# Another order of steps in both attention layers and in the third mixer, and transpositions in place of identity matmuls for spread statistics

## The chip, the cores and the metric

The kernel runs on one core of one Trainium2 chip. The metric is the device time of one execution, in microseconds (us). The core has five engines that run their own instruction streams and meet at semaphores: TensorE (PE; its weight loads are shown apart as PEld), VectorE (DVE), ScalarE (ACT), GpSimd (POOL) and SyncE (SP, which here issues the DMAs). An operand of a matmul lies in SBUF, its result in a bank of PSUM.

## What is computed

Two transformer blocks over 256 tokens of width 1024, in float32. The first has two layers; the token mixer of each holds a banded attention (a), a sparse attention with compressed keys, chosen blocks and a window (b), and a gated delta rule (c). The second has a spatial gate beside a dilated attention, a cross attention to a memory of 256 rows, and a feed-forward network on either side.

```python
def hybrid_layer(x, c, ...):
    mod = jax.nn.silu(c) @ ada_w + ada_b
    sh_m, sc_m, gt_m, sh_f, sc_f, gt_f = jnp.split(mod[:, None, :], 6, axis=-1)
    h = rms_norm(x, norm_mix) * (1 + sc_m) + sh_m
    ...
    o_a = banded_attention(...)
    o_b = nsa_mixer(...)
    o_c = gated_delta_net(cqkv, ca, cb, cz, conv_w, A_log, dt_bias, gdn_norm)
    x = x + gt_m * (jnp.concatenate([o_a, o_b, o_c], axis=-1) @ w_out)
    h = rms_norm(x, norm_ffn) * (1 + sc_f) + sh_f
    gate, up = jnp.split(h @ w_gate_up, 2, axis=-1)
    return x + gt_f * ((jax.nn.silu(gate) * up) @ w_down)
...
def second_block(x, mem, positions, ...):
    h = rmsnorm(x, ffn1_norm[l])
    x = x + 0.5 * swiglu(h, ffn1_w_gate[l], ffn1_w_up[l], ffn1_w_down[l])
    h = rmsnorm(x, mix_norm[l])
    z = h @ w_in[l]
    ...
    y_a = chunked_spatial_gating(z_sgu, sgu_ln_g[l], sgu_ln_b[l], sgu_w_s[l], sgu_b_s[l])
    y_b = dilated_mixture_attention(q, k, v).reshape(b, s, D_ATT)
    y = jnp.concatenate([rmsnorm(y_a, out_norm_a[l]), rmsnorm(y_b, out_norm_b[l])], axis=-1)
    x = x + y @ w_out[l]
    ...
```

## The kernel before

**Projections.** The weights lie in memory as float32 blocks (`in_wbig`). SP fetches one block after another into a few buffers named `raw`; ACT rounds it to `hi` (L397), DVE takes the rest as `lo` (L398), and every product is made of three matmuls, hi by hi, hi by lo and lo by hi (`mm3`, L440, which issues through `mm`, L438). The activations are kept as such a pair too (`hhi`, `hlo`), transposed, with tokens along the free axis. Projections write PSUM tiles named `psw`, the rest `psb` and `psi`.

**Norms.** Squares are summed by one-column matmuls (`sqs`), DVE and POOL turn the sums into reciprocal roots (`rstd`, L456: L458 on DVE, the power L459 on POOL, tile `trs`), and `spread` (L529) lays the two columns of 128 tokens out over all 128 partitions: each column, broadcast along the free axis, is the stationary operand of a 128x128 float32 matmul by the identity. The result scales the blocks of the next norm (`norm_block`, L541). It runs eight times: in the start for the memory and the first norm, at the three feed-forward networks that use it, before the second layer, and twice around 815 us for the second block (once on a tile `r`).

**The conditioning vector.** `c_row` (L677) does the same with the eight columns of `ccol` in the start, for the row that DVE multiplies into the weights of `ada` (L685, L689; these products are spread over layers 0 and 1).

**The attention layers.** `mixer` (L804) writes each part as a generator of steps and runs them in the order of a string, `SEQ` (L275; `next(steps[c])` at L913). The letters: 0 to 3 heads of the delta rule up to its triangular system, t the token-wise projections, i the rounds of the triangular inverse, x and y the two halves of `delta_out` (L1049), c the compression, r the rotations (`rope`, L1166), m the compressed branch (L1223), a the banded attention (`window`, L1261), b the chosen and windowed branch (`selected`, L1326), z the projection `gated` (L874) with the norm of the delta rule's output behind it, p the output projection, A the products of `ada`, L loads of constants and v a value projection of the memory. In `window` the probabilities `sa` are divided by their sums on DVE (L1295) and transposed (L446); `selected` does so with `sb` (L1360); both are then copied out of PSUM on ACT (L1302, L1311, L1373, L1380) and multiplied by the values. `delta_out` ends with a norm (tile `so`: L1089, L458, the power L459 on POOL, L1091) and a copy by ACT to `oc` (L1095).

The order of the string is not the engines' order as such. It is the order in which instructions are written, and with it the order in which buffers and PSUM banks are handed out. A scheduler then places each instruction on its engine as its model thinks its operands ready, with the earlier written first. The orders below are the outcome.

**The third mixer.** `mixer2` (L1490) does the same with another string (L1667): g a projection with gelu or the values, a scores, b transposition of probabilities, p values, s the spatial gate, k the key's rotation, t the transposition of the gate's half. There PE's order is fixed to the written one (`pe_order`).

## Time and profile before

| | |
|---|---|
| runs | 1369.58, 1364.94, 1365.35 us |
| median | 1365.35 us |
| the profiled execution's own time | 1370.71 us |
| its span | 1368.9 us |
| mean granted clock of TensorE | 0.988 |
| DVE busy | 984.0 us (72%) |
| ACT busy | 723.1 us (53%) |
| POOL busy | 42.6 us (3%) |
| DMA, mean | 202 GB/s |

The profile's own execution is the longest of those shown. What is read from it is set against its own 1370.71 us; 1.8 us of that lie outside the span. In rows of a timeline a matmul's duration reaches beyond the start of the next one, since matmuls are pipelined; the pace is read from start to start. A name that is repeated behind an arrow (`psi<-constt,trs`) is output, then stationary and moving operand; `constt` holds the identity and other constants.

### The profile page before, as it was taken

What the parts mean: (1) busy time and instruction counts of PE and PEld (TensorE: products, weight loads), DVE (VectorE), ACT (ScalarE), POOL (GpSimd) and SP (SyncE); (2) the same over time, 40 slices, a digit from 0 to 9 for tenths busy, and PEclk for the clock granted to TensorE, in tenths of its full rate; (3) what the DMA queues carried; (4) which work ended last, traced back from release to release, by engine and by line L of the source; (5) the groups of instructions that cost most, each with busy time, mean ns of one, the idle gap of its engine ahead of it and who ended that gap; (6) DMA issues with size and microseconds to landing.
All of it is one profiled execution on the core that took longest, in us unless ns stands there. A gap on an engine that the chain in (4) does not pass through costs nothing.

```text
span 1368.9 us, 27046 instructions
## 1 busy us (share of the span) xinstructions
PE 1319.0 (96%) x10952; PEld 1261.3 (92%) x10952; DVE 984.0 (72%) x1817; ACT 723.1 (53%) x1349; POOL 42.6 (3%) x47
## 2 busy tenths in 40 slices
PE   6899999999999999999999999999999999999998
PEld 5888879999999988799999989999987999999997
DVE  6878887999886888657666676665676664655554
ACT  4486384655445853855444454444466654544442
POOL 1001000000000000000000000000001000000000
PEclk9999999999999999899999999999999999999999
DMA  8876747799984564147666535555653543555551
GB/s 281 308 266 218 286 153 289 270 346 330 305 276 141 180 213 151 63 139 235 199 215 214 186 129 195 185 185 185 208 184 130 200 156 108 169 185 185 185 185 47
DMA packets 79037, 276.75 MB, mean 202 GB/s; under 512 B 9152, under 2 KB 9920, under 8 KB 78912
## 3 DMA queue, kind: packets, MB, share of 16 engines
q1 hardware_dynamic: 78912, 275.02, 58.7%
q8 instruction: 86, 1.41, 0.4%
q14 instruction: 39, 0.32, 0.1%
HBM read 271.31 MB, written 3.15 MB: 200 GB/s over the span
## 4 chain that ended last, share of the span: by engine, by line
PE 67%; issue 15%; DVE 7%; ACT 5%; DMA 4%; POOL 2%; SPq 0%; DVEq 0%; POOLq 0%; ACTq 0%
PE psw L438 40%; PE psb L438 21%; DMA raw<-in_wbig_dram 3%; PE psi L438 2%; PE psb L446 2%; DVE lo L398 2%; PE psi L1008 1%; DVE raw L689 1%; ACT hi L397 1%; POOL trs L459 1%; DVE hlo L558 1%; ACT s L1628 1%; DMA xres<-in_x_dram 1%; DVE xres L714 0%; PE psb L1131 0%
## 5 line engine op out<-in xcount | busy, mean ns | idle before, releaser
L398 DVE TENSOR_TENSOR lo<-raw,hi 128x1024 fp32r<-128x1024 f32 (+1 forms) x392 | 476.5, 1219 | 189.2 <-ACT hi L397 179.6
L397 ACT ACTIVATE hi<-raw 128x1024 fp32r<-128x1024 f32 (+1 forms) x392 | 409.6, 1052 | 346.7 <-PE psw L438 185.7
L438 PE MATMUL psw<-hhi,hi 128*128 128x256 f32 (+1 forms) x1744 | 499.4, 287 | 3.9 <-ACT hi L397 2.6
L438 PE MATMUL psw<-hhi,lo 128*128 128x256 f32 (+1 forms) x1744 | 497.2, 286 | 1.0 <-DVE lo L398 1.0
L438 PE MATMUL psw<-hlo,hi 128*128 128x256 f32 (+1 forms) x1744 | 497.1, 285 | 0.2 <-DVE hlo L558 0.2
L438 PEld LDWEIGHTS psw<-hhi,hi 128*128 128x128 f32 x1744 | 332.3, 191 | 6.8 <-ACT hi L397 3.5
L438 PEld LDWEIGHTS psw<-hhi,lo 128*128 128x128 f32 x1744 | 332.8, 191 | 2.5 <-DVE lo L398 1.9
L438 PEld LDWEIGHTS psw<-hlo,hi 128*128 128x128 f32 x1744 | 333.4, 191 | 1.5 <-DVE hlo L558 0.6
L438 PE MATMUL psb<-fhi,lo 128*128 128x256 f32 x704 | 197.1, 282 | 0.0
L438 PE MATMUL psb<-flo,hi 128*128 128x256 f32 x704 | 196.9, 281 | 0.0
L438 PE MATMUL psb<-fhi,hi 128*128 128x256 f32 x704 | 194.9, 282 | 0.1
L438 PEld LDWEIGHTS psb<-flo,hi 128*128 128x128 f32 x704 | 133.1, 189 | 0.2
L438 PEld LDWEIGHTS psb<-fhi,lo 128*128 128x128 f32 x704 | 132.8, 189 | 0.0
L438 PEld LDWEIGHTS psb<-fhi,hi 128*128 128x128 f32 x704 | 131.3, 189 | 0.9 <-ACT fhi L478 0.9
L689 DVE CUSTOM_DVE_ANT_0 raw<-raw,constt 128x1024 f32<-128x1024 f32 x96 | 116.2, 1218 | 0.0
L478 ACT ACTIVATE fhi<-fa 128x256 fp32r<-128x256 f32 x88 | 36.7, 417 | 112.3 <-DVE fa L758 59.5
L438 PE MATMUL psb<-oT,hi 128*128 128x256 f32 x512 | 92.7, 283 | 0.0
L438 PEld LDWEIGHTS psb<-oT,hi 128*128 128x128 f32 x512 | 79.0, 189 | 0.3
L438 PE MATMUL psb<-oT,lo 128*128 128x256 f32 x256 | 71.9, 281 | 0.0
L438 PE MATMUL psw<-lo,hhi 128*128 128x256 f32 (+2 forms) x208 | 68.8, 332 | 0.8 <-DVE lo L398 0.8
L438 PE MATMUL psw<-hi,hhi 128*128 128x256 f32 (+2 forms) x208 | 69.5, 336 | 0.0
L438 PE MATMUL psw<-hi,hlo 128*128 128x256 f32 (+2 forms) x208 | 67.9, 329 | 0.0
(364 smaller groups left out, 1549.2 us busy)
## 6 DMA issues: line engine op xcount, KB each, us to landing
raw<-in_wbig_dram SPq DMA_DIRECT2D x498, 512.0 KB, 4.3
mem<-in_mem_dram SPq DMA_DIRECT2D x8, 256.0 KB, 6.6
raw<-in_wbig_dram SPq DMA_DIRECT2D x4, 414.0 KB, 3.4
xres<-in_x_dram SPq DMA_DIRECT2D x4, 256.0 KB, 6.6
memd<-memk SPq DMA_DIRECT2D x4, 256.0 KB, 7.8
mk<-memd SPq DMA_DIRECT2D x4, 256.0 KB, 4.9
mv<-memd SPq DMA_DIRECT2D x2, 512.0 KB, 6.8
out_dram<-out SPq DMA_DIRECT2D x4, 256.0 KB, 2.5
```

Of the source, the lines that this page charges most:

```text
L397: a = self.nc.scalar.activation(hi[:, :n], r, AF.Copy)
L398: d = self.nc.vector.tensor_tensor(lo[:, :n], r, hi[:, :n].bitcast(F32), op=OP.subtract)
L438: return self.pe(self.nc.tensor.matmul(out, lhsT, rhs, start=start, stop=stop))
L446: self.pe(self.nc.tensor.transpose(out, in_, self.cc("ident")))
L459: self.nc.gpsimd.tensor_tensor(dst, dst, self.mhalf[:, :n], op=OP.pow)
L478: self.nc.scalar.activation(hi, src, AF.Copy)
L558: self.nc.vector.scalar_tensor_tensor(lo(m), x, s, hi(m).bitcast(F32), op0=OP.mult, op1=OP.subtract))
L689: self.ada_last = self.nc.vector.tensor_tensor_reduce(w, w, self.crow, 1.0, 0.0, OP.mult, OP.add, m[:, j:j + 1])
L1008: self.pe(self.nc.tensor.matmul(out[h, uh[u]], lhsT(h, u), rhs[h, uh[u]], start=True, stop=True, tile_position=(h.start, h.start)))
L1628: last["exp"] = act.activation(s2[:, o], s2[:, o], AF.Exp, bias=mx[:, i:i + 1], accum_out=sums[t][:, h:h + 1])
```

## The change

Three edits: the two strings of `SEQ`; `mm(..., ident)` against `tr` in `spread` and `c_row`, so that the broadcast column becomes the input of a TensorE transposition with the identity, the instruction that L446 issues elsewhere; and the string of `mixer2`.

```diff
-SEQ = {0: "0tLtttt0t001L11L12012223323A33iiiiciiiiiiciiicixyxycrcxyrArrAAAxyrrAArrmrabbAaaaabbbmbbbbAbbbzzAAzzAAzzApppAApApApAApAAAA",
-       1: "vtttvtv0vtt000111021122333332c2iciiiiiiiiiriiicicrrxyrrrrxyxyaxyacrrbmmbaAbaAAAbAbAzAbabAbzzbbbzzbzppppppp"}
+SEQ = {0: "0tLtttt0t001L11L12012223323A33iiiiciiiiiiciiicixyxyccyxrryrAAxrrrAAAArrmrabbabAaaabbbbmbbAbbzzbAAzzAAzzAppApAApApAApAAAAp",
+       1: "tvvtttv0vtt000111021221233332c3iciiiiiiiiiriiicicrrxyrrxyrraxyxyacrrbmmbaAbaAbAbAAAzAbabAbzzbbbzzbppzppppp"}
...
     def spread(self, r):
...
         p = self.pi()
         for t in range(2):
-            self.mm(p[:, t * 128:t * 128 + 128], r[:, t:t + 1].to_broadcast([128, 128]), self.cc("ident"))
+            self.tr(p[:, t * 128:t * 128 + 128], r[:, t:t + 1].to_broadcast([128, 128]))
...
     def c_row(self):
...
-                self.mm(p[:, i * 128:i * 128 + 128], self.ccol[:, 4 * h + i:4 * h + i + 1].to_broadcast([128, 128]), self.cc("ident"))
+                self.tr(p[:, i * 128:i * 128 + 128], self.ccol[:, 4 * h + i:4 * h + i + 1].to_broadcast([128, 128]))
...
-        for c in "ggkgggagagagabgbsgabgabsgbgtbpp":
+        for c in "ggggkgagagagabsgabgbgabsggbbptp":
```

Three places show how the engines' orders move. A number behind a name tells buffers apart and is not the same before and after.

The first is on PE, behind `delta_out` in layer 1 (about 559 to 571 us of the profile before). `kb,qb` are scores of the selected branch, `sa` and `sb` the transpositions, `psw<-hhi` and `psw<-hlo` the z projection. Before:

```order
L438 MATMUL psb_7168<-kb_7070,qb_7077 128x512
L438 MATMUL psb_7169<-kb_7070,qb_7077 128x512
L446 MATMUL psb_7184<-constt,sa_1451_6953 128x128
L446 MATMUL psb_7184<-constt,sa_7030 128x128
L446 MATMUL psb_7184<-constt,sa_1451_6953 128x128
L446 MATMUL psb_7184<-constt,sa_7030 128x128
L438 MATMUL psb_7215<-kb_7070,qb_7077 128x512
L438 MATMUL psb_7216<-kb_7070,qb_7077 128x512
L446 MATMUL psb_7299<-constt,sb_7085 128x128
L438 MATMUL psw_7235<-hlo_5454,hi_7318 128x256
```

After:

```order
L438 MATMUL psb_7209<-kb_7070,qb_7077 128x512
L438 MATMUL psb_7210<-kb_7070,qb_7077 128x512
L438 MATMUL psw_7235<-hhi_5453,hi_7238 128x256
L438 MATMUL psw_7235<-hlo_5454,hi_7238 128x256
L438 MATMUL psw_7235<-hhi_5453,lo_7239 128x256
L438 MATMUL psw_7235<-hhi_5453,hi_7238 128x256
L438 MATMUL psw_7235<-hlo_5454,hi_7238 128x256
L438 MATMUL psw_7235<-hhi_5453,lo_7239 128x256
L438 MATMUL psb_7281<-k0T_7163,vt_5504 64x256 x2
L438 MATMUL psb_7281<-k1T_7151,vt_5504 64x128 x2
L446 MATMUL psb_7299<-constt,sb_7085 128x128
L438 MATMUL psw_7235<-hhi_5453,hi_7318 128x256
```

Between the last scores and the first `sb` there were no matmuls of the projection, and now there are six, with the product of `k0T` and `k1T`. Of the 28 that were issued ahead of `delta_out`, 13 stay there, 5 lie inside it and the rest behind. The eight small products of the compressed keys (`kcf,qc`) that stood ahead of `delta_out` now stand right behind it.

The second is on PE, behind `delta_out` in layer 0 (about 188 to 194 us of the profile before). Before, transpositions of `sa` alternate with the z projection:

```order
L446 MATMUL psb_2306<-constt,sa_2279 128x128
L438 MATMUL psw_2461<-hlo_672,hi_2464 128x256
L438 MATMUL psw_2461<-hhi_671,lo_2465 128x256
L446 MATMUL psb_2313<-constt,sa_2282 128x128
L446 MATMUL psb_2313<-constt,sa_484_2208 128x128
L446 MATMUL psb_2313<-constt,sa_2282 128x128
L438 MATMUL psw_2461<-hhi_671,hi_2464 128x256
L438 MATMUL psw_2461<-hlo_672,hi_2464 128x256
```

After, from the last products of `delta_out` on:

```order
L438 MATMUL psi_1986<-u_370_1785,qk_729 128x128
L446 MATMUL psb_2316<-constt,sa_2276 128x128 x2
L446 MATMUL psb_2322<-constt,sa_2276 128x128
L446 MATMUL psb_2316<-constt,sa_2279 128x128
L446 MATMUL psb_2322<-constt,sa_483_2205 128x128
L446 MATMUL psb_2316<-constt,sa_2279 128x128
L446 MATMUL psb_2322<-constt,sa_2276 128x128
L446 MATMUL psb_2329<-constt,sa_2279 128x128
L446 MATMUL psb_2329<-constt,sa_484_2208 128x128
L446 MATMUL psb_2329<-constt,sa_2279 128x128
L446 MATMUL psb_2387<-constt,sb_2300 128x128
L438 MATMUL psw_2449<-hhi_671,lo_2453 128x256
```

All transpositions of `sa` stand in one run now. Behind them come nine matmuls of the projection, and then a run of eight transpositions of `sb`: the first four read `sb_2231` and `sb_2300`, the fifth `sb_2347`.

The third is DVE's order at the same place, which makes `sa` and `sb` ready. Before:

```order
L1295 TENSOR_SCALAR sa_2279<-sa_2279,sm_2271 128x256
L1091 SCALAR_TENSOR_TENSOR so_2014<-so_2014,rr_154_733 128x4
L458 TENSOR_SCALAR so_2038<-so_2038 128x4
L1295 TENSOR_SCALAR sa_2279<-sa_2279,sm_2271 128x256
L1091 SCALAR_TENSOR_TENSOR so_2038<-so_2038,rr_161_740 128x4
L1295 TENSOR_SCALAR sa_2282<-sa_2282,sm_2271 128x256 x2
```

After:

```order
L1295 TENSOR_SCALAR sa_2276<-sa_2276,sm_2268 128x256 x2
L1295 TENSOR_SCALAR sa_2279<-sa_2279,sm_2268 128x256 x2
L1089 TENSOR_TENSOR so_1931<-so_1931,so_412_1932 128x4
L1358 TENSOR_TENSOR smb_2302<-smb_2302,sg_723 128x2
L1356 RECIPROCAL smb_2349<-smb_2349 128x2
L458 TENSOR_SCALAR so_1931<-so_1931 128x4
L1360 TENSOR_SCALAR sb_2300<-sb_2300,smb_2302 128x256
L1091 SCALAR_TENSOR_TENSOR so_1931<-so_1931,rr_161_740 128x4
L1360 TENSOR_SCALAR sb_2300<-sb_2300,smb_2302 128x256
L1358 TENSOR_TENSOR smb_2349<-smb_2349,sg_723 128x2
L689 ISA raw_2526,mod_97<-raw_2526,constt 128x1024
L689 ISA mod_97 128x1
```

The four divisions of `sa` no longer stand between the steps of the norm `so`; the divisions of `sb` do (L1360), and one of the large products of `ada` (L689) and the next row of `so` stand ahead of the first division of `sb_2347`.

## Prediction

> **What bounds the kernel now.** First the page: busy time by engine, and the clock that TensorE was granted in 40 slices.
>
> ```profile
> PE 1319.0 (96%) x10952; PEld 1261.3 (92%) x10952; DVE 984.0 (72%) x1817; ACT 723.1 (53%) x1349; POOL 42.6 (3%) x47
> PEclk9999999999999999899999999999999999999999
> ```
>
> PE is busy for 1319.0 of 1368.9 us. All that the change can win back lies in the 49.9 us between, in PE work that becomes cheaper, and in stretches at a lower clock. Next the busy time of the engines by stretch (the columns are the stretch, its length, busy time and count of PE, PEld, DVE, ACT and POOL, the granted clock, the DMA share and GB/s): layer 0's attention, layer 1's, the end of it, and the third mixer.
>
> ```profile
> 60.00:216.00 156.00, 148.43 (x1412) 129.13 (x1412) 128.68 (x350) 105.71 (x263) 7.73 (x8) 1.00 0.67 233
> 440.00:560.00 120.00, 117.01 (x1201) 107.08 (x1201) 101.30 (x254) 73.04 (x184) 5.50 (x5) 1.00 0.53 177
> 560.00:575.00 15.00, 11.94 (x52) 7.15 (x52) 10.61 (x69) 11.61 (x48) 1.49 (x2) 0.66 0.03 12
> 1005.00:1081.00 76.00, 73.66 (x407) 60.41 (x405) 54.45 (x129) 53.09 (x100) 6.68 (x7) 1.00 0.47 159
> ```
>
> The reordered stages leave PE idle for 7.6 us (layer 0), 3.0 and 3.1 us (layer 1) and 2.3 us (third mixer), 16 us in all, and only the 15 us from 560 on run at a low clock. Then PE's waits by what ended them: total, times, longest.
>
> ```profile
> PE psi L438 <- POOL trs L459: 9.5, 7, 2.0
> ...
> PE psb L446 <- ACT s L1628: 0.8, 1, 0.8
> PE psb L446 <- ACT va L1566: 0.6, 1, 0.6
> ```
>
> The largest, the wait for the power on POOL, stands ahead of `spread`, and a transposition waits for it as a matmul does. I count it as unchanged.
>
> **The spreads.** These are the rows of PE (start, duration) at three of the eight, with the row behind each. Those at 250 and 621 us are like the first, the one at 1173 like the second; the last two lie in the start, where PE waits for weights.
>
> ```profile
> 440.03 0.71 PE L438 MATMUL psi<-constt,trs 128*128 128x128 f32 x4 [1.60 <-POOL trs L459]
> 440.50 0.36 PE L438 MATMUL psw<-oT,lo 128*128 128x256 f32 x1
> ...
> 814.93 1.22 PE L438 MATMUL psi<-constt,trs 128*128 128x128 f32 x4 [1.50 <-POOL trs L459]
> 815.80 0.56 PE L438 MATMUL psw<-hhi,lo 128*128 128x256 f32 x1
> ...
> 821.68 0.61 PE L438 MATMUL psi<-constt,r 128*128 128x128 f32 x4
> 822.04 0.36 PE L438 MATMUL psw<-hlo,hi 128*128 128x256 f32 x1
> ```
>
> Two matmuls of a spread leave four records: float32 goes through in two passes. From its start to the next matmul a spread takes 0.47 us at full pace (0.36 at 821.68), and 0.87 where PE runs at half pace. A transposition of a float32 block leaves one record:
>
> ```profile
> L446 PE MATMUL psb<-constt,sb x48: 270/273/448, 189.2 to 583.4; 128*128 128x128 f32 x48
> 194.00 0.71 PE L446 MATMUL psb<-constt,sb 128*128 128x128 f32 x5
> ```
>
> Five take 0.71, one 0.27, so the pace is (0.71 - 0.27) / 4 = 0.11 us, that of one pass: 0.47 / 4 = 0.12. Two transpositions replace four passes, and each spread falls to half. At full pace that saves (3 x 0.47 + 0.36) / 2 = 0.88 us, at half pace 2 x 0.87 / 2 = 0.87. Behind each stands a projection matmul on a PE that is never idle long, so this is on the path: **-1.8 us**. The bounds are 0, if a transposition of a broadcast column takes two passes after all, and -2.7 us, if the two in the start, at 0.87 each, count as well.
>
> **The conditioning vector.** Eight matmuls in 16 passes, and the row behind them:
>
> ```profile
> 8.97 3.75 PE L438 MATMUL psb<-constt,ccol 128*128 128x128 f32 x16 [8.97 <-DMA constt<-in_consts_dram]
> 13.14 0.58 PE L438 MATMUL psw<-oT,hi 128*128 128x256 f32 x1 [0.42 <-ACT hi L397]
> ```
>
> Half of 3.75 is 1.9 us of PE time, but the matmul behind waits for ACT's `hi`, so what hides this edit is the first weight's load and split. I take 0. If that cover went, it would be -1.9; of ACT's two copies of the result one stands behind that `hi` now, and if it comes ahead of it, `hi` is late by 0.6:
>
> ```profile
> 12.05 1.04 ACT L397 ACTIVATE hi<-raw 128x1024 fp32r<-128x1024 f32 x1
> 13.00 0.58 ACT L683 ACTIVATE constt<-psb 128x512 f32<-128x512 f32 x1
> ```
>
> **Layer 1.** The rows of PE behind `delta_out`, the place whose orders are shown with the change:
>
> ```profile
> 560.33 0.93 PE L446 MATMUL psb<-constt,sa 128*128 128x128 f32 x7
> 561.90 1.91 PE L438 MATMUL psb<-kb,qb 64*128 64x512 f32 x4 [0.64 <-ACT oc L1095]
> 565.42 1.11 PE L446 MATMUL psb<-constt,sa 128*128 128x128 f32 x4 [1.61 <-ACT oc L1095]
> 566.47 2.08 PE L438 MATMUL psb<-kb,qb 64*128 64x512 f32 x4
> 569.36 0.45 PE L446 MATMUL psb<-constt,sb 128*128 128x128 f32 x1 [0.81 <-DVE sb L1360]
> ...
> 570.03 0.42 PE L438 MATMUL psw<-hhi,hi 128*128 128x256 f32 x1
> 570.24 0.41 PE L438 MATMUL psw<-hlo,hi 128*128 128x256 f32 x1
> ```
>
> Three waits add up to 3.06 us, and the projection goes at 0.21 us a matmul, half its pace elsewhere. What the projection issued earlier (28 matmuls ahead of `delta_out`) is missing here. The change keeps 15 of them back. At full pace a matmul of it takes 0.12 us from start to start:
>
> ```profile
> 199.07 0.28 PE L438 MATMUL psw<-hhi,lo 128*128 128x256 f32 x1
> 199.19 0.28 PE L438 MATMUL psw<-hhi,hi 128*128 128x256 f32 x1
> ```
>
> 15 x 0.12 = 1.8 us that are no longer spent ahead of `delta_out`, where the inverse's last rounds have rotations and transpositions for cover instead, and that now fall into 3.06 us of waiting: **-1.8 us**. The wait for `sb` (0.81) is where six of them stand. The two waits for `oc` I leave: they come from ACT, which is busy for 11.61 of these 15 us and gets the same work, and the norm's power on POOL lies on the way. The bounds: with all three waits gone and the clock full, 3.06 us, and from 564.3 to 574.5 half of PE's 8.27 busy us there, 4.1 more, so -7.2; and, if the cover ahead of `delta_out` is too thin, the 1.8 us come back as a wait with half of a like low-clock stretch behind it, +3.5.
>
> ```profile
> 564.30:574.50 10.20, 8.27 (x32) 5.24 (x32) 8.09 (x49) 8.75 (x36) 0.00 (x0) 0.50 0.00 1
> ```
>
> **Layer 0.** First PE's two waits for `sa`:
>
> ```profile
> 191.18 0.33 PE L446 MATMUL psb<-constt,sa 128*128 128x128 f32 x1 [0.57 <-DVE sa L1295]
> 192.54 0.60 PE L446 MATMUL psb<-constt,sa 128*128 128x128 f32 x3 [0.79 <-DVE sa L1295]
> ```
>
> Then DVE's rows behind them, one product of `ada`, and the busy time of a stretch a little later (DVE is the third pair):
>
> ```profile
> 190.63 0.16 DVE L1091 SCALAR_TENSOR_TENSOR so<-so,rr 128x4 f32<-128x4 f32 x1 [0.90 <-POOL so L459]
> 192.14 0.61 DVE L1295 TENSOR_SCALAR sa<-sa,sm 128x256 f32<-128x256 f32 x2
> 198.29 1.21 DVE L689 CUSTOM_DVE_ANT_0 raw<-raw,constt 128x1024 f32<-128x1024 f32 x1
> ```
>
> ```profile
> 196.00:200.00 4.00, 4.00 (x34) 3.04 (x31) 4.00 (x12) 4.00 (x13) 0.00 (x0) 1.00 0.87 304
> ```
>
> DVE stood at L1091 for POOL, with divisions of `sa` queued behind. The change writes these ahead of it: 0.57 + 0.79 = 1.36 us go. What is queued behind L1091 now is `sb_2300`'s second division, then a product of 1.21 us, then `sb_2347`. From the first division of `sa` DVE needs 4 x 0.3 for `sa`, 0.2 for small steps, 0.3 for the first of `sb_2300`, 0.9 at L1091, 0.3, 1.21 and 0.3, in all 4.4 us, before the fifth transposition of PE's run can go. PE has 16 transpositions at 0.11 and nine matmuls at 0.12 ahead of it, 2.8 us, and starts them 0.3 behind DVE: a wait of about 1.3 us. Farther on `sb_2363` is transposed with no matmul of the projection beside it. DVE is busy without a gap there (4.00 of 4.00 us) and its work isn't less, so PE can't be past the last `sb` much sooner than before, whatever it wins at `sa`: a second wait between 0 and 1.9 us, of which I take 0.6, a third, as the 27 matmuls ahead of it are cover. -1.36 + 1.3 + 0.6 = **+0.5 us**. Bounds: -1.4, and +3.0 if the waits are 2.5 (DVE's product and its wait, 0.9 + 1.21, with PE early by 0.4) and 1.9. A rearranged fetch (the second half of a compression weight ahead of two `ada` blocks in SP's queue) falls within these.
>
> **The rest.** In the third mixer transpositions of `s` and the values' projection trade places; its waits of 0.8 and 0.6 can go or double: 0, from -1.4 to +1.4. The first matmuls of the two feed-forward networks behind the layers shift by one to nine places around `sqs`, below 1 us either way.
>
> **The sum**: -1.8 - 1.8 + 0.5 = -3.1. The profiled execution, 1370.71 us, would become 1367.6. It is 5.4 us above the median of the runs shown, 1365.35, and the same -3.1 there gives **1362.2 us**. A measurement of this kernel can tell about 0.5%, 6.8 us, from no change; the forecast is well within that.
>
> **A rule on the clock.** Here is PE in layer 0 where `sa` is transposed between waits:
>
> ```profile
> 190.00:193.00 3.00, 1.65 (x13) 1.18 (x12) 1.44 (x8) 2.13 (x9) 1.60 (x2) 1.00 0.95 343
> 812.00:824.00 12.00, 10.43 (x66) 10.17 (x67) 7.73 (x14) 5.71 (x9) 3.38 (x2) 0.72 0.61 218
> ```
>
> PE is busy for half of these 3 us, some of that with transpositions, and the clock stays at 1.00. The second row is a place where a wait was followed by half pace: 0.28 of 12 us below full, so a price of 3.4 us. The Trainium skill, "TensorE: Matmul & The Clock Gate", Part 4 on the PE-mode transpose, says that a transposition doesn't count as busy PE for the clock gate. By that rule each run of transpositions of this change is like a wait. The row at 190 doesn't bear it out, though it doesn't refute it either, as seven matmuls stand among them.
>
> **The rivals.**
> 1. *Layer 1's low clock goes as well.* Six projection matmuls and the product of `k0T` between the scores and the first `sb` keep PE at work; for it speaks that a third of the stretch's waiting was there; against it, the 1.61 us wait for `oc` that came first, and whose cause stays. Then -7.2 takes the place of -1.8: 1356.8 us. Chance 0.19.
> 2. *Layer 0 turns slower.* One mechanism: DVE divides `sb` behind the norm's wait for POOL and the products of `ada`, and PE comes to the new runs of transpositions with nothing else to issue. It decides from the point where PE gets there over 1.5 us ahead of DVE, about what preceded the half pace at 814.93. Then 2.5 and 1.9 us of waits, less 1.4, are +3.0, and two stretches at half pace add 6.8; layer 1 gains nothing: 1365.35 - 1.8 + 3.0 + 6.8 = 1373.4. For it: DVE's 4.4 us against PE's 2.8. Against it: DVE often runs ahead of PE there. Chance 0.10.
> 3. *Runs of transpositions lower the clock.* With one stretch at half pace in layer 0 and no new wait, 1362.2 + 3.4 = 1365.6 us. Chance 0.07. This is what the skill's rule would bring.
> 4. *The change doesn't do what it says*: a broadcast column is transposed in two passes, as many as before, and the orders only trade one wait for another: 1365.4. Chance 0.12.
> 5. The forecast, from 1359 to 1366: 0.52.
>
> **How the numbers follow.** The likeliest is 1362.2. Leaving out the far tails of rivals 1 and 2 gives 1356 to 1371. Faster by over 0.5% means under 1358.5: rival 1, mostly, with a tail of the forecast, 0.20. Slower by over 0.5% means over 1372.2: most of rival 2 and little beside it, 0.09. The rest is 0.71.
>
> **What would show it.** The spread: two records at L446 in place of four at L438, and 0.24 us (0.44 at half pace) to the next matmul; 0.47 refutes the first term. Layer 1: no wait for `sb` around 566, the projection's matmuls in its place; if the stretch is as long as before, or PE waits between the inverse and `delta_out`, the second term is wrong. Layer 0: no waits for `sa`, one of about 1 us for `sb` some 3 us later; a wait over 2 us, or a granted clock below 1.00 between 190 and 216 us, means rival 2. The forecast is wrong altogether if stretches that it doesn't speak of, the third mixer above all, change by over 1.5 us.

## The result, and the profile after

| | before | after |
|---|---|---|
| median of 4 runs each | 1367.46 us | 1349.07 us (1347.76 to 1350.83) |
| ratio, 95% interval | | 0.9865 (0.9837 to 0.9894) |
| span of the profiled execution | 1368.9 us | 1347.9 us |
| mean granted clock in it | 0.988 | 0.995 |

The kernel became 18.4 us faster, 1.35%. The forecast was 1362.2 us, with a range from 1356 to 1371: the measured time lies below all of it. The page of the changed kernel, its busy time and the granted clock in 40 slices:

```profile
PE 1303.4 (97%) x10928; PEld 1250.6 (93%) x10928; DVE 982.3 (73%) x1817; ACT 723.4 (54%) x1349; POOL 38.9 (3%) x47
PEclk9999999999999999999999999999999999999999
```

DVE and ACT do what they did. PE is busy 15.6 us less although only 24 of its records are gone, and POOL 3.7 us less, which no edit intended. Both are clues: work of the same kind goes faster.

A part of that is TensorE's clock. In every trace it stands at half for stretches of 3.41 us, or two or three times that, and at full otherwise. Ahead of PE's last matmul such stretches add up to 30.7 us in the profile before and to 10.2 after. Work at half clock takes twice as long, so half of the difference, about 10 of the 21.0 us between the two spans, can be the clock's (less where PE waited in them anyway). A profile is one execution; by the granted clock that is recorded for each, (1 - clock) x span fell from 15.8 us (11 of the kernel before, mean clock 0.9885) to 7.6 (six of the changed kernel, 0.9943, run e16 below): up to 8 us.

This table of PE's time from one spread to the next, read from the start of their rows in both traces, says where the 21.0 us are:

| stretch | before | after | difference |
|---|---|---|---|
| layer 0, attention | 214.5 | 208.3 | -6.2 |
| first network, up to layer 1's norm | 189.9 | 189.5 | -0.4 |
| layer 1, attention | 181.1 | 173.9 | -7.2 |
| second network | 193.8 | 193.6 | -0.2 |
| between the spreads at 815 and 822 us | 6.8 | 5.6 | -1.2 |
| third network, third mixer, cross attention | 350.9 | 348.4 | -2.4 |
| last network to PE's last matmul | 189.7 | 186.6 | -3.1 |

Apart from the last spread's passes the last network and the stretch ahead of it were in no term of the forecast; a change of over 1.5 us in such a stretch was one of its own signs of being wrong. PE's waits after the change, of the kinds that the prediction spoke of (total, times, longest):

```profile
PE psi L446 <- POOL trs L459: 7.8, 7, 1.6
...
PE psb L446 <- DVE sb L1360: 0.9, 1, 0.9
```

The waits for `sa` (L1295) and for `oc` (L1095) are in no row any more. Two places that were forecast, a spread and the conditioning vector, each with the row behind it (start, duration):

```profile
433.55 0.43 PE L446 MATMUL psi<-constt,trs 128*128 128x128 f32 x2 [0.94 <-POOL trs L459]
433.74 0.37 PE L438 MATMUL psw<-oT,hi 128*128 128x256 f32 x1
```

```profile
9.75 1.94 PE L446 MATMUL psb<-constt,ccol 128*128 128x128 f32 x8 [9.75 <-ACT oT L557]
14.53 0.80 PE L438 MATMUL psw<-oT,hi 128*128 128x256 f32 x2 [2.84 <-ACT hi L397]
```

A spread has two records and takes 0.19 us to the next matmul, where it took 0.47. `c_row` has halved to 1.94, and the wait for `hi` behind it has grown from 0.42 to 2.84: that gain is hidden, as said.

### The profile page after: what moved, and what is told of

It reads as the page before. It is cut to its first block, busy times and chain, and to the rows that moved or that the text cites. A ratio compares the mean times of both kernels' runs of the same rounds, so it can differ in the third digit from the quotient of the medians.

```text
span 1347.9 us, 26975 instructions
## 1 busy us (share of the span) xinstructions
PE 1303.4 (97%) x10928; PEld 1250.6 (93%) x10928; DVE 982.3 (73%) x1817; ACT 723.4 (54%) x1349; POOL 38.9 (3%) x47
## 4 chain that ended last, share of the span: by engine, by line
PE 67%; issue 16%; DVE 8%; ACT 5%; DMA 2%; POOL 2%; SPq 0%; POOLq 0%; DVEq 0%; ACTq 0%
PE psw L438 40%; PE psb L438 22%; DVE lo L398 2%; PE psi L438 2%; PE psb L446 1%; DMA raw<-in_wbig_dram 1%; PE psi L1008 1%; ACT hi L397 1%; POOL trs L459 1%; DVE raw L689 1%; DVE xres L714 1%; DVE hlo L558 1%; DVE conv L938 1%; PE psb L1131 1%; DMA mem<-in_mem_dram 0%
## 5 line engine op out<-in xcount | busy, mean ns | idle before, releaser
L689 DVE CUSTOM_DVE_ANT_0 raw<-raw,constt 128x1024 f32<-128x1024 f32 x96 | 116.3, 1218 | 0.2 <-DMA raw<-in_wbig_dram 0.2
```

What stands on the lines that cost most here:

```text
L689: self.ada_last = self.nc.vector.tensor_tensor_reduce(w, w, self.crow, 1.0, 0.0, OP.mult, OP.add, m[:, j:j + 1])
```

## The experiments: each part alone, and all without it

**The transpositions alone.**

```diff
-self.mm(p[:, t * 128:t * 128 + 128], r[:, t:t + 1].to_broadcast([128, 128]), self.cc("ident"))
+self.tr(p[:, t * 128:t * 128 + 128], r[:, t:t + 1].to_broadcast([128, 128]))
...
-self.mm(p[:, i * 128:i * 128 + 128], self.ccol[...].to_broadcast([128, 128]), self.cc("ident"))
+self.tr(p[:, i * 128:i * 128 + 128], self.ccol[...].to_broadcast([128, 128]))
```

> The two edits from an identity matmul to a transposition (spread and c_row) alone, the three strings as before. Theory A (the direct saving, and an indirect one): -1.8 us of PE time, and at the last spread (1172 us) DVE's order changes with the edit: a multiplication that needs the spread stands ahead of the second split, so POOL's power is no longer beside two splits; it takes 1.6 instead of 2.75 us, PE waits 1.1 us less, and the half-pace stretch behind it (2.6 us lost) is gone: -1.8 - 1.1 - 2.6 = about -5 us. Theory B (the saving is only the passes, the clock stretch there is luck): -1.8 us or less, POOL's power as long as before.

**Each string alone**: layer 0's, layer 1's and the third mixer's, with the line of the change.

```diff
-SEQ = {0: "0tLtttt0t001L11L12012223323A33iiiiciiiiiiciiicixyxycrcxyrArrAAAxyrrAArrmrabbAaaaabbbmbbbbAbbbzzAAzzAAzzApppAApApApAApAAAA",
+SEQ = {0: "0tLtttt0t001L11L12012223323A33iiiiciiiiiiciiicixyxyccyxrryrAAxrrrAAAArrmrabbabAaaabbbbmbbAbbzzbAAzzAAzzAppApAApApAApAAAAp",
```

```diff
-       1: "vtttvtv0vtt000111021122333332c2iciiiiiiiiiriiicicrrxyrrrrxyxyaxyacrrbmmbaAbaAAAbAbAzAbabAbzzbbbzzbzppppppp"}
+       1: "tvvtttv0vtt000111021221233332c3iciiiiiiiiiriiicicrrxyrrxyrraxyxyacrrbmmbaAbaAbAbAAAzAbabAbzzbbbzzbppzppppp"}
```

```diff
-        for c in "ggkgggagagagabgbsgabgabsgbgtbpp":
+        for c in "ggggkgagagagabsgabgbgabsggbbptp":
```

> The string of layer 0 alone. Theory A (each stage's gain belongs to its own string): the stretch from the first norm's spread to the next one gets 5 to 6 us shorter, the whole kernel -5 to -6 us. Theory B (what layer 0 won came from the transpositions ahead of and behind it, as the prediction's walk through the string has it): between -1 and +1 us.

> The string of layer 1 alone. Theory A (moved matmuls cover the waits and the clock stays at full pace): -7 us, of which 3.5 from the half-pace stretch that is gone. Theory B (the clock stretch is set by where an idle gap falls on the clock's own grid, so with all earlier times as before it is still there): -3 to -4 us.

> The string of the third mixer alone. Theory A: -2 us, from the waits at 1051 and 1069 us. Theory B (the waits only move): within 1 us of no change; the 2.4 us that this stretch lost in the changed kernel came from elsewhere.

**All but one part, and a pair**: the same lines again. e6 is the changed kernel with the `-` line of layer 0's string back, e7 with the two `-` lines of the transpositions, e8 with that of the third mixer and e10 with that of layer 1; e9 is the kernel before with the `+` lines of both layers.

> The changed kernel with the old string for layer 0. Alone the four parts gave -5.0 (transpositions), -2.8 (layer 0), -6.0 (layer 1) and +1.4 us (third mixer), together -12.4, and the change -18.4. Theory A (the parts add up, and the 6 us between are scatter of runs): 2 to 4 us slower than the changed kernel, 1351 to 1353 us. Theory B (layer 0's gain is offset alone by half-pace stretches elsewhere, as its lower granted clock, 0.987, says, and not in the changed kernel): 6 to 8 us slower, 1355 to 1357 us.

> All three strings, without the transpositions. Theory A (additive): 5 us slower than the changed kernel, 1354 us. Theory B (the transpositions make the others' gain possible, by other half-pace stretches): 8 us or more slower, 1357 us or over.

> The changed kernel with the old string for the third mixer. Theory A (additive, that string does nothing or costs 1 us): 1347 to 1349 us, the same as the changed kernel or faster. Theory B (in the changed kernel that string is worth the 2.4 us that its stretch is shorter): 1351 to 1352 us.

> The strings of both layers, without the third mixer's and without the transpositions. Alone they gave -2.8 and -6.0 us in the medians; all three strings together -16.0, with the third mixer's alone at nothing. Theory A (additive, and the three strings' -16.0 owed to the third mixer's in their company): -9 us, 1359 us. Theory B (the two layers' strings are worth more together, in half-pace stretches that either brings alone): -14 to -16 us, 1352 to 1354 us.

> The changed kernel with the old string for layer 1. Theory A (additive; layer 1 alone gave -6.0): 1355 us. Theory B (the layer's stretch is 7.2 us shorter in every profile with its string, and what the sum of the parts lacks belongs to it as well): 1357 to 1360 us, and the half-pace stretch of about 7 to 10 us at the end of layer 1 is back.

Measured, as medians and ratios to runs of the kernel before on the same chip:

| run | us | ratio (95%) |
|---|---|---|
| e1, transpositions | 1362.51 | 0.9966 (0.9953 to 0.998) |
| e2, layer 0 | 1364.75 | 0.9981 (0.9968 to 0.9994) |
| e3, layer 1 | 1361.51 | 0.9955 (0.9942 to 0.9969) |
| e4, third mixer | 1368.91 | 1.0004 (0.9989 to 1.0019) |
| e6, all but layer 0 | 1354.23 | 0.9901 (0.9883 to 0.9919) |
| e7, all but transpositions | 1352.02 | 0.9884 (0.9866 to 0.9902) |
| e8, all but third mixer | 1348.75 | 0.9862 (0.9843 to 0.9881) |
| e9, both layers | 1350.24 | 0.9874 (0.9853 to 0.9894) |
| e10, all but layer 1 | 1353.81 | 0.9892 (0.9873 to 0.9911) |

Each of three parts is worth 3 to 6 us alone or taken out last; the third mixer's string is worth nothing in either. The prediction had -1.8 for the transpositions, +0.5 for layer 0, -1.8 for layer 1 and 0. By the medians they measured -5.0 alone and -3.0 as the last part (e7), layer 0 -2.8 and -5.2 (e6), layer 1 -6.0 and -4.7 (e10), the third mixer +1.4 and +0.3 (e8).

So the parts don't add up: alone they sum to -12.4 us, and together they give -18.4. The two layers' strings show it best, -2.8 and -6.0 alone and -18.0 together (e9, by its ratio -17.2), more than either theory said. By the clocks most of the surplus can be half pace. The same (1 - clock) x span, as a mean over the executions, is 14.2 us for the kernel before, 17.7 in e2 and 12.0 in e3; in e9 it is 8.9, against 15.2 for the kernel before on that chip. Alone the two strings would change it by +1.3 us, and together they change it by -6.2. One reason why e2 is so poor in this is shown below.

e1's -5.0 is that of its first theory, e3's -6.0 lies nearer to its first, and e2's -2.8 between its two. e4 and e8 bear out that the third mixer's string does nothing. e6, e7 and e10 came out at 1354.23, 1352.02 and 1353.81 us: e6 between its two theories, e7 below both, e10 nearest to the additive one. e10's other theory also said that the half pace at the end of layer 1 would be back with the old string; it was not, as shown below.

## The experiments: what each part is made of

**Why transpositions are worth more than their PE time.** At the last spread, POOL's power and what DVE does beside it, before and then after:

```profile
1169.74 2.75 POOL L459 TENSOR_TENSOR trs<-trs,mhalf 128x2 f32<-128x2 f32 x1 [53.08 <-DVE trs L458]
```

```profile
1169.58 2.35 DVE L398 TENSOR_TENSOR lo<-raw,hi 128x1024 fp32r<-128x1024 f32 x2
1174.22 0.69 DVE L753 TENSOR_TENSOR gu<-psw,R 128x512 f32<-128x512 f32 x1 [2.29 <-ACT R L734]
```

```profile
1153.35 1.61 POOL L459 TENSOR_TENSOR trs<-trs,mhalf 128x2 f32<-128x2 f32 x1 [53.82 <-DVE trs L458]
...
1341.18 0.70 POOL L459 TENSOR_TENSOR trs<-trs,mhalf 128x2 f32<-128x2 f32 x1 [186.22 <-DVE trs L458]
```

```profile
1153.19 1.22 DVE L398 TENSOR_TENSOR lo<-raw,hi 128x1024 fp32r<-128x1024 f32 x1
1155.90 0.69 DVE L753 TENSOR_TENSOR gu<-psw,R 128x512 f32<-128x512 f32 x1 [1.50 <-ACT R L734]
1156.51 2.35 DVE L398 TENSOR_TENSOR lo<-raw,hi 128x1024 fp32r<-128x1024 f32 x2
```

The same instruction on two columns takes 0.70 us with DVE free (the last row of POOL), 1.61 beside one split of a weight and 2.75 beside two: it ends about 0.55 us behind the last split beside it (1169.58 + 2.35 and 1153.19 + 1.22), as if it began only then. With the cheaper spread the scheduler puts the product L753 ahead of the second split. The Trainium skill, "SBUF — State Buffer", section "Who interferes with whom", says that a DVE instruction with two SBUF inputs contends with a GpSimd instruction that reads SBUF, and that the ports they share are an exclusive lock. The rows agree. To try this alone, e5 leaves the kernel before as it is but for one order on DVE: the second split waits for the first L753 of the last network.

```diff
-        self.split_last = d
+        self.split_last, self.guard = d, self.guard and self.order(d, self.guard)
...
+            self.guard = self.gu[3, 0] if (b, f) == (3, 1) else None
```

> The kernel before with one order added: in the last feed-forward network the split of the third weight block (L398 on DVE) stands behind the first multiplication that needs the spread (L753), as it does by itself in the run with the transpositions alone. Nothing else of the change. Theory A (POOL's power waits while DVE's splits run, and the wait it makes for PE brings the half pace): the power at the last spread takes 1.6 us instead of 2.75, PE's wait there about 1.0 instead of 2.2, the 2.6 us of half pace behind it are gone: -3 to -4 us. Theory B (the power's time there isn't DVE's doing): still 2.75 us, no change.

It measured 1365.43 us, ratio 0.9979 (0.9965 to 0.9992), and its power takes what the theory says:

```profile
1168.50 1.61 POOL L459 TENSOR_TENSOR trs<-trs,mhalf 128x2 f32<-128x2 f32 x1 [54.73 <-DVE trs L458]
```

That is -2.6 us, a little less than the theory's 3 to 4 (by the interval between -1.1 and -4.8), of the transpositions' -5.0. Part is PE's wait, which is 1.1 us shorter (2.0 and 0.9 us in the traces). The rest fits the clock behind it, as e5's profile has no half pace there. It shows in these two rows of busy time (of the kernel before and of the changed one, seven us from the spread on; the clock stands behind POOL's pair):

```profile
1173.00:1180.00 7.00, 7.00 (x40) 7.00 (x40) 2.34 (x3) 4.28 (x6) 0.00 (x0) 0.59 0.62 224
```

```profile
1155.00:1162.00 7.00, 6.98 (x59) 6.99 (x59) 5.39 (x8) 5.66 (x8) 0.00 (x0) 1.00 0.75 262
```

The long wait doesn't always bring the half pace. Of the 12 profiles in which the power takes 2.75 us, 8 have half pace behind it, and e7, e9, e13 and e14 have none: from the last spread to PE's last matmul takes 186.9 us in these four, and 189.6 or 189.7 in e3, e4 and the kernel before. None of the 8 profiles with a shorter power has it. So the passes (1.8 us) and the wait (1.1) make 2.9 us, which is what the kernel loses without the transpositions in e7 (3.0), whose profile has no half pace there; where it comes, the part is worth more, as in e1.

**Layer 1.** Of its string e11 takes only the piece with the last two heads' steps and the compression.

```diff
-1: "vtttvtv0vtt000111021122333332c2iciiiiiiiiiriiicicrr...
+1: "vtttvtv0vtt000111021221233332c3iciiiiiiiiiriiicicrr...
```

> One piece of the string of layer 1 alone: the steps of the four heads and the compression, 122333332c2 to 221233332c3, so that head 2 comes before head 1's step and head 3, not head 2, is last. PE's order at delta_out (13 projection matmuls ahead, 5 in it, six between the scores and the first sb) is that of the whole string. Theory A (this piece holds the projection's matmuls back, and that is what layer 1 won): -5 to -6 us, the layer's stretch 6 to 7 us shorter, no wait for oc. Theory B (the pieces behind it, with delta_out ahead of the rotations and the later ada steps, matter as much): -2 to -3 us.

It measured 1365.58 us, ratio 0.9977 (0.9963 to 0.9991): -2.7 us, as its second theory said, though no wait for `oc` is left, as the first one did. Layer 1 takes 176.8 us in it, 175.0 in e3, 173.9 after and 181.1 before. The place behind `delta_out` in the changed kernel, PE's rows without the projection's:

```profile
548.75 0.33 PE L446 MATMUL psb<-constt,sa 128*128 128x128 f32 x1
...
554.54 0.44 PE L446 MATMUL psb<-constt,pcm 128*128 128x128 f32 x2 [1.26 <-DVE pcm L1252]
...
558.12 0.33 PE L446 MATMUL psb<-constt,sb 128*128 128x128 f32 x1
```

One wait of 1.26 us stands where there were three of 3.06, and the clock stays full; these are the busy times there (changed kernel, then e11):

```profile
545.00:560.00 15.00, 13.67 (x102) 9.69 (x100) 10.70 (x71) 13.24 (x59) 2.02 (x2) 1.00 0.04 14
```

```profile
545.00:575.00 30.00, 28.68 (x239) 24.14 (x238) 20.64 (x103) 27.14 (x104) 2.01 (x2) 1.00 0.17 54
```

This looks like rival 1 with its price, -7.2 us, but it is two things. The clock is at half for 10.2 us at that place in the profile before, which costs 5.1 of the 7.2; what is left, 2.1 us, is about what the waits lost (3.06 - 1.26 = 1.8). And the half pace does not follow from the waits alone. e1 has the old string and the same three waits, and runs at full clock there:

```profile
559.37 1.91 PE L438 MATMUL psb<-kb,qb 64*128 64x512 f32 x4 [0.64 <-ACT oc L1095]
562.89 0.66 PE L446 MATMUL psb<-constt,sa 128*128 128x128 f32 x4 [1.61 <-ACT oc L1095]
565.42 0.30 PE L446 MATMUL psb<-constt,sb 128*128 128x128 f32 x1 [0.81 <-DVE sb L1360]
```

```profile
550.00:575.00 25.00, 21.94 (x165) 17.41 (x165) 15.14 (x83) 22.78 (x82) 2.01 (x2) 1.00 0.14 45
```

e10 is like it. Of the eleven profiles with the old string of layer 1 nine have half pace behind `delta_out`, for 6.8 or 10.2 us, all but e1 and e10; of the nine with the new one, or with e11's piece of it, none has. So the new order keeps the half pace away, and the old one brings it often, but not always. The traces give a hint why: within each of them all half-clock stretches begin and end on one grid of 3.41 us (before, they begin at 35.22, 55.70, 564.28, 813.46 and 1171.85, whole multiples of 3.41 apart), and this grid lies otherwise against the kernel in each execution. Whether a wait brings half pace may depend on how it lies on the grid; no run tests that.

The one piece removes the waits for `oc`. What the others add (2.9 us of the stretch, 1.7 of it a half-clock stretch at its start in e11) was not taken apart further.

**Layer 0, by its pieces.** e12 takes the piece around `delta_out`, e14 that with a and b, e13 the last steps of the projection and of `ada`.

```diff
-...ixyxycrcxyrArrAAAxyrrAArrmrabbA...
+...ixyxyccyxrryrAAxrrrAAAArrmrabbA...
```

```diff
-...rabbAaaaabbbmbbbbAbbbzzAAzz...
+...rabbabAaaabbbbmbbAbbzzbAAzz...
```

```diff
-...AAzzApppAApApApAApAAAA",
+...AAzzAppApAApApAApAAAAp",
```

> One piece of the string of layer 0 alone: the order of delta_out, rotations and ada behind the inverse (rcxyrArrAAAxyrr to cyxrryrAAxrrrAA), with the attention's steps as before. Theory A (layer 0's gain is the norm of delta_out out of the way of the divisions of sa): the layer's stretch 4 to 6 us shorter as with the whole string, -3 us in all. Theory B (the gain is in the a and b steps, or in the fetch): within 1 us of no change.

> Only the last piece of layer 0's string, the order of the output projection's last steps and the products of ada (p and A). Theory: this piece alone gives the shorter stretch from the last output projection matmul to the spread behind it, 11.97 us before, 9.16 in the changed kernel, because PE's two idle us there shrink to 0.8; so 9.2 us in that stretch and about 2.8 us off the time, a ratio of 0.998. Rival: the stretch only shifts idle time to the feed-forward network's first projection behind the spread, and the time stays, within 1 us.

> Only the piece of layer 0's string with a, b and z behind the delta rule's output. From the delta rule's first product of that part to the first output projection matmul PE takes 35.2 us before, 31.8 in the changed kernel and 33.5 with the delta_out piece alone. Theory: the two pieces add, so 33.4 us here, and about 1.7 us off the time; the float32 products of values and keys stand in longer runs, with fewer turns between them and the projection. Rival: the pieces work only together (the first decides which buffers come free for the second), 35 us here and no difference.

e12 measured 1368.22 us, ratio 0.9996 (0.9981 to 1.0011); e13 1366.22, 0.9982 (0.9969 to 0.9996); e14 1367.76, 0.9987 (0.9972 to 1.0003). So e13 did what its theory says, and e12 and e14 can't be told from no change. From the delta rule's first product (`psi<-X,kd`) to the first output projection matmul PE takes 35.2 us before, 31.8 after, 33.5 in e12 and 34.8 in e14; e14's stretch shrank by a quarter of what was expected of it. From the last output projection matmul to the spread it takes 12.0 before, 9.2 after and 9.6 in e13. These two stretches are all that the string wins: from the first product to the next spread it is 69.9 us before and 63.7 to 64.3 in all eight profiles with the new string.

The second of the two is DVE's. Its last product of `ada` and the first row of the residual behind it, before and after, and then PE's last matmul of the output projection in either:

```profile
235.61 1.22 DVE L689 CUSTOM_DVE_ANT_0 raw<-raw,constt 128x1024 f32<-128x1024 f32 x1
...
237.18 0.48 DVE L714 SCALAR_TENSOR_TENSOR xres<-psb,mod,xres 128x256 f32<-128x256 f32 x1
```

```profile
222.79 1.23 DVE L689 CUSTOM_DVE_ANT_0 raw<-raw,constt 128x1024 f32<-128x1024 f32 x1 [0.21 <-DMA raw<-in_wbig_dram]
...
230.93 0.88 DVE L714 SCALAR_TENSOR_TENSOR xres<-psb,mod,xres 128x256 f32<-128x256 f32 x2
```

```profile
238.14 0.28 PE L438 MATMUL psb<-oT,lo 128*128 128x256 f32 x1
```

```profile
234.89 0.28 PE L438 MATMUL psb<-oT,lo 128*128 128x256 f32 x1
```

Before, four products of `ada` stood last and DVE came to the residual 1.0 us ahead of PE's end; now a step of the projection stands last, and DVE is there 4.0 us ahead of it. PE had waited there for what DVE and ACT make behind the residual, and in the changed kernel no row between that end and the spread has a wait. The longer waits before:

```profile
PE psw L438 <- DVE lo L398: 0.5, 1, 0.5
PE psw L438 <- ACT hi L397: 0.4, 1, 0.4
```

The first stretch, 3.4 us shorter, is hardly explained by idle time: the waits that rows print in it add up to 1.7 us before and 1.4 after. Some 1.3 us of work moved ahead of it (a score product and two transpositions), and the remaining 1.8 us are in small gaps that no row prints as a wait. Were they the turns between kinds of matmul? u1 appends runs and turns behind the kernel's last matmuls: transpositions (T), projection matmuls (R) and 128x128 float32 products (F).

```diff
+            self.pe_order = True
...
+            for k, n in ("R", 64), ("T", 16), ("R", 16), ("TR", 16), ("F", 16), ("R", 16), ("FR", 16), ("T", 16), ("F", 16), ("TF", 16), ("R", 16):
+                for i in range(n):
+                    for c in k:
+                        one(c, i)
```

> The kernel before with work added behind its output products: runs of PE instructions that wait for nothing, each kind 16 times in a run and then in turns: transpositions of float32 (T), projection matmuls of rounded float32 128x256 (R) and float32 products 128x128 in two passes (F). Theory, from layer 0's rows: a T with an R costs the same in turns as in runs, 0.109 + 0.119 = 0.23 us a pair; an R with an F costs 0.34 us a pair in runs and about 0.55 in turns, since the step from F to R took 0.31 us and that from R to F 0.21; a T with an F 0.33 in runs and 0.4 or more in turns. Rival: turns cost nothing between any kinds (0.34 and 0.33), and the shorter stretch of layer 0 has another source.

```profile
1368.63 1.91 PE L446 MATMUL psb<-constt,xres 128*128 128x128 f32 x16
1370.29 2.14 PE L438 MATMUL psw<-hlo,hhi 128*128 128x256 f32 x16
1372.27 0.27 PE L446 MATMUL psb<-constt,xres 128*128 128x128 f32 x1
...
1375.97 3.74 PE L438 MATMUL psb<-constt,xres 128*128 128x128 f32 x32
1379.46 2.18 PE L438 MATMUL psw<-hlo,hhi 128*128 128x256 f32 x16
1381.48 0.39 PE L438 MATMUL psb<-constt,xres 128*128 128x128 f32 x2
...
1386.93 1.91 PE L446 MATMUL psb<-constt,xres 128*128 128x128 f32 x16
```

Sixteen T and sixteen R take 1372.27 - 1368.63 = 3.64 us in runs and 1375.97 - 1372.27 = 3.70 in turns; F and R 5.51 and 5.45. These turns are free, and the theory fell. But the shapes were not those of layer 0, whose products with values have a stationary block of 128x64 (`128*64` in a row). (Behind a row's arrow the moving operand stands first and the stationary one second, not the other way round as the section on the profile before has it: `psw<-hlo,hhi` here comes from a call with `hhi` as the stationary operand.) u2 takes these, by 256 columns (G) and by 128 (H).

```diff
+                elif c == "G":
+                    self.mm(p[:64, j * 256:j * 256 + 256], x[:, 64:128], self.xk(7))
...
+            for k, n in ("R", 64), ("G", 16), ("R", 16), ("GR", 16), ("H", 16), ("R", 16), ("HR", 16), ("T", 16), ("G", 16), ("TG", 16), ("GH", 16), ("R", 16):
```

> As the first measurement of turns, with the shapes that layer 0 turns between, which the first one did not hold: float32 products of a 128x64 stationary block by 256 columns (G) and by 128 columns (H), with projection matmuls (R) and transpositions (T). Theory: it is these shapes that make a turn dear, since in layer 0 the step from pcT by vcmp to a projection matmul took 0.31 us and the next projection step 0.22, so a G with an R costs about 0.2 us a pair more in turns than in runs. Rival: turns cost nothing here either (within 0.02 us a pair); then what layer 0 lost in small gaps before was short waits for operands or banks, which the orders took away.

```profile
1370.34 7.12 PE L438 MATMUL psb<-xres 128*64 128x256 f32 x32
1377.39 2.19 PE L438 MATMUL psw<-hlo,hhi 128*128 128x256 f32 x16
1379.50 0.65 PE L438 MATMUL psb<-xres 128*64 128x256 f32 x2
...
1393.74 3.71 PE L438 MATMUL psb<-constt,xres 128*64 128x128 f32 x32
1397.38 2.16 PE L438 MATMUL psw<-hlo,hhi 128*128 128x256 f32 x16
...
1432.80 0.38 PE L438 MATMUL psb<-constt,xres 128*64 128x128 f32 x2
...
1442.55 0.38 PE L438 MATMUL psb<-constt,xres 128*64 128x128 f32 x2
```

In runs G and R take 1379.50 - 1370.34 = 9.16 us, in turns 1393.74 - 1379.50 = 14.24: 0.32 us more for each pair, where the theory said 0.2, and 0.16 for each turn. G and H, which have the same tile shape, take 9.75 us for fifteen pairs in turns, 0.65 each, and in runs 7.05 / 16 + 3.64 / 16 = 0.67: nothing for a turn. So it is not the kind that costs but the change of the array's tile shape. The Trainium skill, "TensorEngine Tiling (Array Packing)", section "Key Properties", says that changing the tiling mode drains TensorE; u2 fits that and gives a price, 0.16 us (64x128 and smaller blocks, which the layers have too, were not run). By the traces' rows, layer 0 has 59 changes of tile shape before and 44 after. Behind the delta rule's first product there are 18 before and 6 after, and 10 of these 12 are between 128x64 and 128x128: 1.6 us, or 1.9 at the same price for all 12, an estimate, against the 1.8 us in small gaps. The pieces fit less well. For e14, with 16 changes, 0.3 us were due, and its stretch is 0.4 shorter than before. For e12, with 14, 0.3 to 0.6 were due, and of the 1.7 us that its stretch lost, all but 0.1 is the moved work and the waits. Small gaps have other sources too, which stay open. The two pieces mostly work together: 14 and 16 changes alone, 6 with both.

**What took layer 0's gain back in e2 and e12.** ACT loads a function table ahead of the exponential of the third mixer. Its row before and in e2:

```profile
1046.89 1.28 ACT L1628 ACT_TABLE_LOAD   x1
...
1051.87 0.40 ACT L1628 ACTIVATE s<-s,mx 128x128 f32<-128x128 f32 x1 [3.70 <-DVE mx L1626]
```

```profile
1044.15 1.28 ACT L1628 ACT_TABLE_LOAD   x1 [5.11 <-DVE mx L1626]
```

In e2 and e12 the load itself waits for DVE and then takes its 1.28 us on the path; PE's wait for `s` goes from 0.8 to 2.2, half pace follows, and the stretch of the third network, third mixer and cross attention is 353.1 and 353.2 us there, 350.9 in the kernel before and 348.4 to 351.1 in the other runs. No edit of theirs touches it. This is read from the traces; no run changes the load alone.

**A version that goes on.** e15 orders, in every network, two weight splits on DVE behind the first product, as e5 did for one; e16 is the changed kernel once more.

```diff
-        self.split_last = d
+        self.split_last = d; self.guard and self.order(d, self.guard.pop())
...
+            self.guard = [gu] * 2 if f == 0 else self.guard; w = self.weight(("dn", b, f))
```

> The changed kernel, with one more order: in every feed-forward network the two weight splits that DVE writes behind the first gated product wait for that product, so that no split lies beside the power on POOL at the spread of the second block and of the last network. Theory: the power then takes 0.70 us instead of 1.61 there, PE's wait at the last spread goes from 1.04 to about 0.1, and the time is 1 to 2 us below the changed kernel's 1349.07. Rival: the splits come too late instead, PE waits for lo by 1 us or more in these networks, and the time is the same or up to 2 us longer.

> The changed kernel once more, unedited, to weigh the run with the added order, 1346.07 us. Theory: the added order is worth 2 to 3 us, so this kernel repeats 1349 (1348 to 1350.5), ratio 0.9865. Rival: most of those 3 us is the spread between runs of layer 0's first part, where the two kernels have the same orders and yet 3.8 us less was seen; then this comes out at 1346.0 to 1347.5, ratio 0.984, and layer 0 takes about 205 us in its profile as it did there.

e15 measured 1346.07 us (1345.62 to 1346.73), ratio 0.983 (0.9813 to 0.9848); e16 1350.01 (1344.3 to 1353.63), 0.9855 (0.9828 to 0.9882). The power takes 0.70 us at the last spread, as it should, and PE has no wait there; at the first spread of the second block it still takes 1.62, and PE waits 1.50 us, so that half of the edit's aim was missed:

```profile
1150.23 0.70 POOL L459 TENSOR_TENSOR trs<-trs,mhalf 128x2 f32<-128x2 f32 x1 [54.32 <-DVE trs L458]
```

But from the first spread of the second block to PE's last matmul e15's profile is only 0.5 us shorter than the changed kernel's, while layer 0, whose orders are the same, takes 204.5 us there, 208.3 in the profile after and 210.0 in e16's, nearly all of it ahead of the delta rule, where ACT waits for weights. e16 repeats the changed kernel's time, as its theory said. e15's median is the lowest of all; whether more than 0.5 us of that is its own stays open.

## Why the prediction was wrong

The sum counted PE's passes and PE's waits in the reordered places, and put the clock at nothing. The prediction names stretches at a lower clock among what can be won, but prices them only in rivals. Up to 8 us of the gain are there, by the recorded clocks. The terms one by one:

1. *Spreads, -1.8.* The pace was right: 0.19 us at 433.55, two records. What failed is "I count it as unchanged", said of PE's wait for POOL. The scheduler placed DVE's splits anew, and of PE's 2.0 us at the last spread 1.1 were owed to the second split. With the passes that is 2.9 us, and 3.0 is what e7 lost; the rest of e1's 5.0 comes and goes with the half pace. The wait at 440 us went from 1.60 to 0.94 as well, in the profiles with layer 1's string.
2. *The conditioning vector, 0.* Right: the wait behind it grew by what it saved.
3. *Layer 1, -1.8.* Projection matmuls came into the waiting, as said, but "the two waits for `oc` I leave" was wrong: all three waits of 3.06 us went, and a new one of 1.26 for `pcm` came. Without the clock the stretch is 2.1 us shorter, near the forecast, in part by luck, as other waits went than were said. The term failed by the half pace, another 5.1 us in this pair of profiles. The text had that as rival 1 with a chance of 0.19, and that the stretch then shows just the rival's 7.2 is luck: the rival made it of 3.06 and 4.1. Why the waits for `oc` went is not settled beyond this: the heads' piece alone removes them.
4. *Layer 0, +0.5.* The waits were nearly as forecast: those for `sa` gone (1.36), one for `sb` of 0.9 where 1.3 was said, and not the second one of 0.6. What failed is that the sum held waits alone. Changes of tile shape (1.6 to 1.9 us) were in no term, since no row prints them; nor was 1.3 us of work that moved ahead of the delta rule, where ACT waits for weights; and the stretch at the network's start, put at "below 1 us either way", gave 2.8. In all it is -6.1.
5. *Third mixer, 0.* Right, e4 and e8.
6. *Rivals.* The fourth is refuted by the spread's two records, the second by layer 0's shorter stretch. The third did not come true either: there is no half pace in layer 0 where transpositions stand in runs, as the busy time of the changed kernel there shows.

```profile
186.00:200.00 14.00, 12.94 (x112) 11.31 (x112) 12.12 (x36) 12.73 (x49) 2.28 (x3) 1.00 0.67 215
```

Ten transpositions of `sa` in a run and a wait of 0.9 us lie in these 14 us, and the clock is 1.00. That alone would not refute the rule that the prediction quotes from the Trainium skill, "TensorE: Matmul & The Clock Gate", Part 4, as e1 shows that waits too can leave the clock at 1.00. The profile of the kernel before has a plainer place, in the third mixer, where PE does nothing but transpose and wait for 2.6 us (to 1071.82). Eleven profiles have such a run, and in all of them the clock is full there and behind it, while the wait of 2.0 us ahead of the last spread brought half pace in 8 of 12:

```profile
1069.21 0.60 PE L446 MATMUL psb<-constt,s 128*128 128x128 f32 x4
1069.64 0.38 PE L446 MATMUL psb<-constt,y 128*128 128x128 f32 x2
1070.67 0.88 PE L446 MATMUL psb<-constt,y 128*128 128x128 f32 x6 [0.65 <-ACT va L1566]
1071.38 0.60 PE L446 MATMUL psb<-constt,s 128*128 128x128 f32 x4
```

```profile
1069.45:1072.86 3.41, 2.76 (x26) 2.53 (x25) 1.71 (x2) 3.41 (x7) 0.00 (x0) 1.00 0.74 243
```

With these sizes the sum would have been -1.8 (passes) - 1.1 - 0.7 (waits for POOL) - 2.1 (layer 1) - 6.1 (layer 0) = -11.8 us, and with up to 8 for the clock some -20, against the 18.4 measured. What sets the half-clock stretches is the part that stays open.

## What to carry to other kernels

Count the changes of TensorE's tile shape in an order before and after it is changed: at 0.16 us each (128x64 against 128x128) they show as no wait, and products with narrow blocks are best written in one run. Compare the granted clock of many executions, and not of two profiles, before a gain is put down to an order. Before a wait for POOL is called fixed, look at what DVE does beside it, and before an edit's gain is summed from PE's rows, look at what stands last on DVE ahead of the next norm.

## What the runs showed of the hardware

- The power of two columns on POOL: 0.70, 1.61 and 2.75 us beside none, one and two of DVE's splits of a 128x1024 weight.
- A change of the array's tile shape, 128x64 against 128x128, between float32 products and projection matmuls: 0.16 us; turns between transpositions, rounded and full float32 products of one tile shape: nothing measurable.
- A table load on ACT that waits for the activation's operand itself puts its 1.28 us on the path.
- The clock stands at half in stretches of 3.41 us or two or three times that, on a grid that differs from execution to execution. The same waits (2.0 us at the last spread; 0.64, 1.61 and 0.81 behind `delta_out`) are followed by half pace in some executions and not in others.
- 2.6 us of transpositions and waiting alone left the clock at full.
